# A second product over all 128 partitions: the keys' low part on both halves

## The chip, the cores and the metric

The kernel runs on one core of one Trainium2 chip. The metric is the device time of one execution in microseconds (us), taken several times; times here are those of that one core.

## The reference

Two layers of an encoder trunk over 512 tokens of 1024 channels, in float32. Each layer has two mixers and a channel mixer. Cut to what matters here:

```
z = rms_norm(x) @ w_in          # split into qa ka va, qi ki wi, cq ckv kr, ga gb
# indexer: 8 heads of 64, one shared key
score = sum_h wi[t,h] * relu(qi[t,h] . ki[s]) * scale ; masked by chunks of 64
sel = top_k(score, 128)
# mixer A: 8 heads of 64, RMS-normed queries and keys, softmax over the selected keys
logits = qa[t,h] . ka[s,h] * scale + bias[h, bucket(s - t)]
# mixer B: 8 heads of 96, softmax over all keys of the chunk and before
logits = qb[t,h] . kb[s,h] * scale
x = x + (gate_a * (y_a @ w_proj_a) + gate_b * (y_b @ w_proj_b)) @ w_out
x = x + (silu(conv(gat)) * conv(val)) @ w_down     # of rms_norm(x) @ w_up
```

## The kernel before

Float32 values are split into two parts, a high one (a cast to float32r) and a low one (what is left), and a product of two values is made of several products of parts on TensorE, added up in one PSUM bank. A dense tile of weights takes 24 matmuls of 512 columns (line 513) or 48 of 256 columns (`rows`, line 536).

Weights stream through the class `Weights`: SP's queue loads a raw tile (line 151), ScalarE casts the high part (line 168), VectorE makes the low part (line 177), or a DMA that adds does (line 194). Three raw tiles and four split tiles are held (`WB`). All other operands of 128 x 512 come from one pool of 65 slots.

A layer first computes the projections by tiles as a generator, the filler. Attention work is written as generators too, and `weave` steps them in turn and hands out filler after each step at rates that are constants. VectorE's and ScalarE's follow-up work is put off by `later(n, f)`, where the clock counts steps. So the order of TensorE's work is fixed in the program: in the indexer one step is a head's scores of one query block (two matmuls), then one step of filler (three matmuls). The top-k follows, on VectorE, beside projections and mixer B; then mixer A, four heads a group.

The scores of the indexer and of mixer A use `mm2` (lines 310 to 314). A head's queries are stacked: one half of the 128 partitions holds the high part, the other the low part. The keys' high part stands on both halves, so one product over 128 partitions (line 313) gives high times high plus low times high. The second product (line 314) takes the half that holds the queries' high part, 64 partitions, with the keys' low part on the same half. Which half it is alternates with the head. Widths are 128, 256, 384 and 512 columns by query block in mixer A, and 256, 384 and 512 in the indexer.

The indexer's key (`evac_kiw`, lines 559 to 570) gets its low part on both halves by a VectorE copy (line 569). Mixer A's keys are made in `turn` of `heads` (lines 740 to 756), two heads at a time: ScalarE casts each head's high part on its own half (line 752), a DMA on SP's queue copies it to the other half (line 753), and VectorE makes the low part (line 754) one step later, each head's half into the one tile `kal` of the pair.

Mixer B's scores (lines 1114 to 1116) are three products: high by high over 100 partitions (96 dimensions and 4 that carry the mask), high by low and low by high over 96.

Of the kernel before, what the change touches and what calls it, by code (L numbers as in the profile page):

```python
# [98 lines left out]
def dense_plan():  # L99
    """The weight tiles of a layer in the order of their use: (name, index, columns)."""  # L100
    p = [("qi", m, 1024) for m in range(4)] + [("kiw", 0, 1024)]
    p += [("ckv", j, 1024) for j in range(2)] + [("cq", j, 1024) for j in range(3)]
    p += [("gb", m, 1024) for m in range(GB_0)]
    p += [("kv", 0, 1024), ("uq", 0, 1152)]
    p += [("gb", m, 1024) for m in range(GB_0, GB_1)]
    p += [("kv", 1, 1024), ("uq", 1, 1152)]
    p += [("gb", m, 1024) for m in range(GB_1, 8)]
    for g in range(2):
        p += [(n, 2 * g + half, 1024) for n in ("qa", "ka", "va") for half in range(2)]
        if g == 0:  # L110
            p += [("ga", m, 1024) for m in range(GA_0)]
    p += [("pb", m, 1024) for m in range(4 if PBO == 1 else 0)]
    p += [("ga", m, 1024) for m in range(GA_0, 8)]
    p += [("pb", m, 1024) for m in range(0 if PBO == 1 else 4)] + [("pa", m, 1024) for m in range(4)]
    p += [("wo", m, 1024) for m in range(8)]
    for f0, f1 in FF_PARTS:
        for f in range(f0, f1):
            p += [("uv", f, 1024), ("ug", f, 1024)]
        p += [("dn", 11 * mp + kp, 512) for mp, _, _ in DOWNS[f0] for kp in range(f0 // 2, f1 // 2)]
    return p  # L120
# [7 lines left out]
class Weights:  # L128
    """Streams the dense weights: load, then split into two exact float32r parts."""
# [50 lines left out]
    def split_four(self, i, t, h, o, lag):  # L180
        """Four blocks, 21 11 12 22, to the parts of seven: 11 12 22 and Winograd's four sums."""
        self.sums(i, t)
        self.nc.scalar.copy(h[:, :896], t[:, 128:1024])  # L183
        kp = self.seq[i][1] % 11
        if kp in (DN1 if kp < FS // 2 else DN2):
            self.low_by_dma(t[:, 128:1024], o[:, :896])
            return
        self.later(lag, lambda: self.nc.vector.tensor_tensor(  # L188
            out=o[:, :896], in0=t[:, 128:1024], in1=h[:, :896].bitcast(F32), op=OP.subtract))

    def low_by_dma(self, t, o):
        """The rest of a value, by a DMA that adds it to its first part's negative."""
        self.nc.scalar.activation(o, t, AF.Copy, scale=-1.0)  # L193
        self.nc.gpsimd.dma_start(o.bitcast(F32), t, accum_op=OP.add)  # L194
# [19 lines left out]
    def ahead(self):  # L214
        """Called when the last tile given out has been used: the one after the next takes its place."""
        for j in range(1, WB[1]):
            self.split(self.at + j, 2)
        for j in range(WB[1], WB[1] + WB[0] - 1):
            self.load(self.at + j)
        if PRE and self.at + WB[1] < len(self.seq) and self.seq[self.at + WB[1]][0] == "dn":  # L220
            self.sums(self.at + WB[1], self.raw[self.at + WB[1]])
# [3 lines left out]
def trunk(ctx: ExitStack, tc: tile.TileContext, xT, wd, vecs, rel, rot_n, onehot, outT):  # L225
# [58 lines left out]
    def hi_lo(src, name, scale=None, lag=1):  # L284
        """Splits a whole [128, 512] source into exact parts, with a scale by partition if any."""
        h, o = slot(name + "h", F32R), slot(name + "l", F32R)
        split_into(h, o, src, scale, lag)
        return h, o
# [9 lines left out]
    def stack(p, name):  # L298
        """The parts of two heads of 64, each head's above one another: [high; low] and [low; high]."""
        e, o = slot(name + "e", F32R), slot(name + "o", F32R)  # L300
        A.copy(e[0:64], p[0:64])
        A.copy(o[64:128], p[64:128])

        def low():
            V.tensor_tensor(out=e[64:128], in0=p[0:64], in1=e[0:64].bitcast(F32), op=OP.subtract)
            V.tensor_tensor(out=o[0:64], in0=p[64:128], in1=o[64:128].bitcast(F32), op=OP.subtract)
        later(1, low)
        return e, o

    def mm2(p, q, ts, kk, kl, half, start, stop):  # L310
        """A head's [high; low] queries with its keys: twice the high part, then the low one."""
        r = slice(64 * half, 64 * half + 64)
        mm(p, lhsT=q[:, ts], rhs=kk, start=start, stop=False, skip_group_check=True)  # L313
        mm(p, lhsT=q[r, ts], rhs=kl[r], start=False, stop=stop, skip_group_check=True)  # L314
# [6 lines left out]
    def rsqrt(a, shape, quick=False):  # L321
        """a ** -0.5 by Newton's steps from a first guess by the exponent's bits."""
# [22 lines left out]
    def table(func, out, in_, **kw):  # L345
        """An activation of a function with a table of its own: all of one come before the next one's."""
# [44 lines left out]
    # Columns that mask the later half of a query block's own keys, when they are contracted with each other.  # L391
# [43 lines left out]
    class Norm:  # L435
# [17 lines left out]
        def finish(self, gap):  # L453
            """Mean square plus eps by token, its inverse root, and that over all partitions."""
# [20 lines left out]
        def rescale(self, xs, lag, step):  # L475
            """New parts, of the inputs times their factor."""
# [10 lines left out]
        def after(self, f):  # L487
            """Runs f once the factor is there."""
            if self.waiting is None:
                f()  # L490
            else:
                self.waiting.append(f)
# [26 lines left out]
    def rows(name, grp, nrm, evac):  # L519
        """256 columns of the projection with tokens on partitions; evac(b, p) per two blocks of them."""  # L520
# [29 lines left out]
    def mix_dense(l, nrm):  # L550
        """The dense products of a mixing phase, as the tensor engine's filler."""
# [22 lines left out]
        def turn_wk(wk):  # L574
# [7 lines left out]
            # The indexer's weights by head: |w| and its sign.  # L582
# [12 lines left out]
            # The shared rotary key, turned and scaled.  # L595
# [113 lines left out]
        # Mixer A's queries and keys: by token, normed there, then turned.  # L709
        def heads(name, grp, gain):  # L710
# [30 lines left out]
            def turn(pr):  # L741
# [8 lines left out]
                e, o, low = slot("kae", F32R), slot("kao", F32R), slot("kal", F32R)  # L750
                for t, r, r2 in ((e, slice(0, 64), slice(64, 128)), (o, slice(64, 128), slice(0, 64))):
                    A.activation(t[r], p[r], AF.Copy, scale=gain[r])
                    nc.sync.dma_start(t[r2].bitcast(F32), t[r].bitcast(F32))
                    later(1, lambda t=t, r=r: V.scalar_tensor_tensor(low[r], p[r], gain[r], t[r].bitcast(F32),
                                                                      op0=OP.mult, op1=OP.subtract))
                st["ka"][hd:hd + 2] = (e, low), (o, low)
# [20 lines left out]
        # Mixer B's queries, keys and values of four heads, by token.  # L777
# [156 lines left out]
    class Feeder:  # L934
        """Called after each step of the attention: hands out filler, and side work, at given rates."""
# [25 lines left out]
    def index_scores():  # L961
        st["sc"] = {}
        for i in (3, 2, 1):
# [3 lines left out]
            for h in range(8):  # L967
                p = bank("L")
                ts = slice(i * 128, (i + 1) * 128)
                mm2(p[:, :w], st["qi"][h], ts, st["kih"][:, :w], st["kil"][:, :w], h % 2, True, True)  # L970
# [43 lines left out]
    def values(P, v, half, two):  # L1014
        """v(j): a head's values of key block j, [128 keys, high and low 64]; half: which of the pair's heads."""
# [39 lines left out]
    def bias_a(h):  # L1055
        """A head's bias by distance, and the mask of the keys that were not selected."""
# [12 lines left out]
    def scores_a(h, P):  # L1069
# [5 lines left out]
        for i in range(4):  # L1075
# [3 lines left out]
            mm2(p[:, :w], q, ts, kk[:, :w], kl[:, :w], h % 2, True, not SELPE)  # L1079
# [11 lines left out]
    def turn_b(h):  # L1091
        """A head's queries and keys with their dimensions on partitions."""
# [13 lines left out]
    def scores_b(h, P):  # L1106
# [3 lines left out]
        for i in range(4):  # L1110
# [4 lines left out]
            mm(p[:, :w], lhsT=qh[0:96, ts], rhs=kl[0:96, :w], start=False, stop=False, skip_group_check=True)  # L1115
            mm(p[:, :w], lhsT=ql[0:96, ts], rhs=kh[0:96, :w], start=False, stop=True, skip_group_check=True)
# [6 lines left out]
    def weave(gens, each, others=()):  # L1123
        """Steps the generators in turn, with filler and side work after each step."""
# [33 lines left out]
    for l in range(DEPTH):  # L1158
# [55 lines left out]
        # Mixer B.  # L1214
# [14 lines left out]
        # Mixer A.  # L1229
# [26 lines left out]
        # Gates, output projection.  # L1256
# [25 lines left out]
        # Channel mixer.  # L1282
# [3 lines left out]
        def act_pair(kp, c0, c1):  # L1286
            """The parts of the seven operands of two blocks of the hidden layer, by halves of the tokens."""
# [54 lines left out]
        # Two products a bank; "n" marks an operand, and so a product, of the opposite sign.  # L1342
# [6 lines left out]
        def down(mp, pairs, first, last, then):  # L1349
            """Two blocks of the output: 2 x 2 blocks a time by seven products of Winograd's form of Strassen's."""  # L1350
# [92 lines left out]
def lay_out(i):  # L1443
# [3 lines left out]
    def tiles_t(w):  # L1447
        """[K, 128 columns] -> [128, K]: input blocks beside each other."""
        return w.reshape(-1, 128, w.shape[1]).transpose(1, 0, 2).reshape(128, -1)
# [73 lines left out]
```

## Time and profile before

| what | us |
|---|---|
| median of 3 runs | 1611.2 |
| fastest and slowest of them | 1602.91, 1611.62 |
| the profiled execution, first to last instruction | 1601.6 |
| TensorE (PE) busy | 1584.5 |
| weight loads (PEld) busy | 1339.8 |
| VectorE (DVE) busy | 1117.3 |
| ScalarE (ACT) busy | 953.2 |
| GpSimd (POOL) busy | 413.0 |

The profile is of one execution; its own time is known as the span from its first to its last instruction, and the time outside that span isn't told. Durations of matmuls are modelled at their ends, as matmuls are pipelined: a matmul of 512 columns is shown with about 0.39 us, though the next starts 0.23 us after it. So distances between starts tell TensorE's pace better than durations do. The granted clock of TensorE is 1.000 over the span.

### The profile page before, as it was taken

How to read it: one execution, taken by the hardware profiler on the slowest of the kernel's cores; microseconds unless marked ns; L12 is line 12 of the kernel's file. 1: busy time of each engine (PE TensorE's matmuls, PEld its weight loads, DVE VectorE, ACT ScalarE, POOL GpSimd, SP SyncE). 2: the span in 40 equal slices, each digit the busy share in tenths (PEclk: the TensorE clock that was granted, in tenths of full speed). 3: DMA queues.
4: the chain of work that ended last, by engine and by line, in shares of the span. 5: the costliest groups of instructions: out<-in, count | busy, mean ns of one | idle time of the engine just before them, and what ended most of it. 6: DMA issues, size and time to landing. Idle time of an engine off the chain costs nothing.

```text
span 1601.6 us, 23906 instructions
## 1 busy us (share of the span) xinstructions
PE 1584.5 (99%) x8662; PEld 1339.8 (84%) x8662; DVE 1117.3 (70%) x2271; ACT 953.2 (60%) x1551; POOL 413.0 (26%) x602
## 2 busy tenths in 40 slices
PE   9999999999999999999999999999999999999998
PEld 6688999778888898889976889997788888978898
DVE  7699987656567692547776999876574666825576
ACT  6657676763467545764456576777735675356642
POOL 1235003210012231226801340123000122412276
PEclk9999999999999999999999999999999999999999
DMA  7374122634378538982443731246244884398833
GB/s 239 112 177 119 54 80 80 166 98 145 105 181 194 119 101 206 222 194 81 141 142 80 184 100 53 80 102 162 80 148 120 179 198 108 104 210 202 203 97 105
DMA packets 70983, 219.01 MB, mean 137 GB/s; under 512 B 8192, under 2 KB 8488, under 8 KB 70736
## 3 DMA queue, kind: packets, MB, share of 16 engines
q1 hardware_dynamic: 51968, 147.31, 29.1%
q0 software_dynamic: 18432, 67.38, 22.8%
q10 hardware_dynamic: 464, 2.79, 0.5%
q8 instruction: 68, 1.11, 0.3%
q14 instruction: 51, 0.42, 0.1%
HBM read 143.77 MB, written 6.84 MB: 94 GB/s over the span
## 4 chain that ended last, share of the span: by engine, by line
PE 73%; DVE 7%; POOL 4%; DMA 3%; ACT 2%; issue 2%; POOLq 0%; ACTq 0%; DVEq 0%
PE D L513 37%; PE T L513 14%; PE D L536 7%; PE Y L1030 2%; PE T L1023 2%; DMA wr<-in_wd_dram 2%; PE L L314 2%; POOL wr L205 2%; PE L L1370 2%; PE L L513 1%; DVE wl L188 1%; POOL wr L203 1%; POOL wr L204 1%; PE L L313 1%; DMA wl<-wr 1%
## 5 line engine op out<-in xcount | busy, mean ns | idle before, releaser
L168 ACT CAST wh<-wr 128x1024 fp32r<-128x1024 f32 x202 | 211.8, 1050 | 180.0 <-PE D L513 72.6
L194 POOL DMA_DIRECT2D wl<-wr x128 | 110.7, 867 | 693.0 <-ACT wl L193 638.4
L513 PE MATMUL D<-hxh,wh 128*128 128x512 f32 x464 | 188.4, 406 | 0.1
L513 PE MATMUL D<-hxl,wh 128*128 128x512 f32 x464 | 187.1, 403 | 0.0
L183 ACT CAST wh<-wr 128x896 fp32r<-128x896 f32 x88 | 82.8, 942 | 128.0 <-POOL wr L205 96.9
L193 ACT ACTIVATE wl<-wr 128x1024 fp32r<-128x1024 f32 (+1 forms) x128 | 135.7, 1061 | 30.5 <-PE D L513 21.2
L205 POOL TENSOR_TENSOR wr<-wr 128x256 f32<-128x256 f32 x88 | 109.4, 1243 | 92.9 <-DVE wr L204 83.2
L188 DVE TENSOR_TENSOR wl<-wr,wh 128x896 fp32r<-128x896 f32 x88 | 101.7, 1156 | 43.8 <-ACT wh L183 35.6
L513 PE MATMUL D<-hxh,wl 128*128 128x512 f32 x464 | 127.9, 401 | 0.0
L1065 POOL TENSOR_TENSOR P<-M,sel 128x128 f32<-128x128 f32 (+1 forms) x64 | 53.0, 883 | 269.3 <-DMA M<-skewd 107.2
L536 PE MATMUL D<-wh,hxh 128*128 128x256 f32 x384 | 115.9, 302 | 0.0
L536 PE MATMUL D<-wl,hxh 128*128 128x256 f32 x384 | 109.0, 284 | 0.0
L536 PE MATMUL D<-wh,hxl 128*128 128x256 f32 x384 | 108.8, 283 | 0.0
L513 PEld LDWEIGHTS D<-hxh,wh 128*128 128x128 f32 x464 | 87.5, 189 | 19.9 <-issue 4.3
L513 PEld LDWEIGHTS D<-hxl,wh 128*128 128x128 f32 x464 | 87.4, 188 | 19.7 <-issue 4.8
L177 DVE TENSOR_TENSOR wl<-wr,wh 128x1024 fp32r<-128x1024 f32 x74 | 92.5, 1253 | 12.0 <-ACT wh L168 9.1
L513 PE MATMUL D<-hrl,wh 128*128 128x512 f32 x256 | 99.6, 389 | 0.0
L513 PE MATMUL T<-hrl,wh 128*128 128x512 f32 x256 | 99.6, 389 | 0.0
L513 PE MATMUL D<-hrh,wh 128*128 128x512 f32 x256 | 99.6, 389 | 0.0
L513 PE MATMUL T<-hrh,wh 128*128 128x512 f32 x256 | 99.6, 389 | 0.0
L513 PEld LDWEIGHTS D<-hxh,wl 128*128 128x128 f32 x464 | 83.8, 188 | 17.5 <-issue 2.0
L293 DVE TENSOR_TENSOR ptl<-T,pth 128x512 fp32r<-128x512 f32 (+3 forms) x128 | 61.5, 486 | 25.6 <-ACT pth L292 24.2
(397 smaller groups left out, 4527.0 us busy)
## 6 DMA issues: line engine op xcount, KB each, us to landing
wr<-in_wd_dram SPq DMA_DIRECT2D x198, 512.0 KB, 4.0
wl<-wr POOLq DMA_DIRECT2D x124, 512.0 KB, 5.4
wr<-in_wd_dram SPq DMA_DIRECT2D x88, 256.0 KB, 2.7
x<-in_xT_dram SPq DMA_DIRECT2D x16, 256.0 KB, 4.9
M<-skewd SPq DMA_DIRECT2D x16, 256.0 KB, 3.9
skewd<-biasd ACTq DMA_DIRECT2D x1, 2560.0 KB, 13.3
wr<-in_wd_dram SPq DMA_DIRECT2D x4, 576.0 KB, 3.7
wl<-wr POOLq DMA_DIRECT2D x4, 576.0 KB, 6.4
```

Source lines behind the costliest of these rows:

```text
L168: self.nc.scalar.copy(h[:, :n], t[:, :n])
L177: eng.tensor_tensor(out=o[:, c], in0=t[:, c], in1=h[:, c].bitcast(F32), op=OP.subtract)
L183: self.nc.scalar.copy(h[:, :896], t[:, 128:1024])
L188: self.later(lag, lambda: self.nc.vector.tensor_tensor(out=o[:, :896], in0=t[:, 128:1024], in1=h[:, :896].bitcast(F32), op=OP.subtract))
L193: self.nc.scalar.activation(o, t, AF.Copy, scale=-1.0)
L194: self.nc.gpsimd.dma_start(o.bitcast(F32), t, accum_op=OP.add)
L205: g(2)(out=b[:, 6:8], in0=b[:, 0:3:2], in1=b[:, 3:6:2], op=OP.add)
L293: later(lag, lambda: V.tensor_tensor(out=o, in0=src, in1=h.bitcast(F32), op=OP.subtract))
L314: mm(p, lhsT=q[r, ts], rhs=kl[r], start=False, stop=stop, skip_group_check=True)
L513: mm(p, lhsT=w, rhs=x, start=n == 0, stop=n == len(seq) - 1, skip_group_check=True)
L536: mm(pp[b][:, t, :], lhsT=x, rhs=w, start=n == 0 and half == 0 and t == 0, stop=n == 11 and half == 1, skip_group_check=True)
L1065: G.tensor_tensor(out=P[:, P0[i]:P0[i] + w], in0=M[:, 512 - w:512], in1=sel[:, SEL0[i]:SEL0[i] + w], op=OP.add)
```

## The change

`mm2` loses its argument `half`, and its second product takes all 128 partitions of queries and keys. With the keys' low part on both halves, this adds the product of the two low parts, which was left out before. In the indexer only the call changes. In mixer A each head gets a low tile of its own, and a DMA copies the low part to the other half. Mixer B's second and third product take 100 partitions instead of 96. The diff, without lines that only drop comments:

```diff
-    def mm2(p, q, ts, kk, kl, half, start, stop):
-        r = slice(64 * half, 64 * half + 64)
+    def mm2(p, q, ts, kk, kl, start, stop):
         mm(p, lhsT=q[:, ts], rhs=kk, start=start, stop=False, skip_group_check=True)
-        mm(p, lhsT=q[r, ts], rhs=kl[r], start=False, stop=stop, skip_group_check=True)
+        mm(p, lhsT=q[:, ts], rhs=kl, start=False, stop=stop, skip_group_check=True)
...
-                e, o, low = slot("kae", F32R), slot("kao", F32R), slot("kal", F32R)
-                for t, r, r2 in ((e, slice(0, 64), slice(64, 128)), (o, slice(64, 128), slice(0, 64))):
+                for i, (r, r2) in enumerate(((slice(0, 64), slice(64, 128)), (slice(64, 128), slice(0, 64)))):
+                    t, low = slot("kah", F32R), slot("kal", F32R)
                     A.activation(t[r], p[r], AF.Copy, scale=gain[r])
                     nc.sync.dma_start(t[r2].bitcast(F32), t[r].bitcast(F32))
-                    later(1, lambda t=t, r=r: V.scalar_tensor_tensor(low[r], p[r], gain[r], t[r].bitcast(F32),
-                                                                      op0=OP.mult, op1=OP.subtract))
-                st["ka"][hd:hd + 2] = (e, low), (o, low)
+
+                    def rest(t=t, low=low, r=r, r2=r2):
+                        V.scalar_tensor_tensor(low[r], p[r], gain[r], t[r].bitcast(F32), op0=OP.mult,
+                                               op1=OP.subtract)
+                        nc.sync.dma_start(low[r2].bitcast(F32), low[r].bitcast(F32))
+                    later(1, rest)
+                    st["ka"][hd + i] = t, low
...
-                mm2(p[:, :w], st["qi"][h], ts, st["kih"][:, :w], st["kil"][:, :w], h % 2, True, True)
+                mm2(p[:, :w], st["qi"][h], ts, st["kih"][:, :w], st["kil"][:, :w], True, True)
...
-            mm2(p[:, :w], q, ts, kk[:, :w], kl[:, :w], h % 2, True, not SELPE)
+            mm2(p[:, :w], q, ts, kk[:, :w], kl[:, :w], True, not SELPE)
...
             mm(p[:, :w], lhsT=qh[0:100, ts], rhs=kh[0:100, :w], start=True, stop=False, skip_group_check=True)
-            mm(p[:, :w], lhsT=qh[0:96, ts], rhs=kl[0:96, :w], start=False, stop=False, skip_group_check=True)
-            mm(p[:, :w], lhsT=ql[0:96, ts], rhs=kh[0:96, :w], start=False, stop=True, skip_group_check=True)
+            mm(p[:, :w], lhsT=qh[0:100, ts], rhs=kl[0:100, :w], start=False, stop=False, skip_group_check=True)
+            mm(p[:, :w], lhsT=ql[0:100, ts], rhs=kh[0:100, :w], start=False, stop=True, skip_group_check=True)
```

## The prediction

> **What bounds the kernel now.** I read the page first (busy time), then the waits of TensorE, then the timeline around the instructions that the diff touches, and last the rows of the engines and queues that could take over.
>
> ```profile
> span 1601.6 us, 23906 instructions
> ...
> PE 1584.5 (99%) x8662; PEld 1339.8 (84%) x8662; DVE 1117.3 (70%) x2271; ACT 953.2 (60%) x1551; POOL 413.0 (26%) x602
> ```
>
> TensorE is busy for 99% of the span, and no other engine comes near. A busy PE is not yet a PE at its peak, so two more questions are needed: does PE wait for anybody, and does it run its matmuls at their usual pace? The longest wait of PE in the whole span is the row below (operation, releaser, us in total, times, longest). The two rows after it are the only waits of PE between 85 and 232 us, from the end of the first layer's indexer to the start of its mixer A.
>
> ```profile
> PE L L317 <- ACT hxh L295: 1.7, 1, 1.7
> ...
> PE L L804 <- DVE vb L293: 0.6, 1, 0.6
> PE T L1099 <- DVE qao L306: 0.2, 1, 0.2
> ```
>
> So PE is the bound, and hardly ever kept waiting. The pace is read from the distance between the starts of neighbouring matmuls, in the timeline (start, duration, operation). First a stretch of the indexer:
>
> ```profile
> 46.53 0.39 PE L513 MATMUL D<-hxh,wh 128*128 128x512 f32 x1
> 46.76 0.39 PE L513 MATMUL D<-hxl,wh 128*128 128x512 f32 x1
> 46.98 0.39 PE L313 MATMUL L<-kih,qio 128*128 128x512 f32 x1
> 47.30 0.49 PE L314 MATMUL L<-kil,qio 64*128 64x512 f32 x1
> 47.72 0.50 PE L513 MATMUL D<-hxh,wh 128*128 128x512 f32 x1
> 48.06 0.40 PE L513 MATMUL D<-hxl,wh 128*128 128x512 f32 x1
> ```
>
> Usual matmuls of 512 columns start 0.23 us apart (46.53, 46.76, 46.98). Around line 314, the one with 64 rows, three distances are longer: 0.32 before it, 0.42 after it, 0.34 after the next. Together 1.08 us instead of 3 x 0.23 = 0.69: 0.39 us are lost to one narrow matmul, though PE counts as busy throughout. Is it the 64 rows, or the accumulation into a bank of tag L? Mixer B's scores answer, which accumulate three products in such a bank, the later two with 96 rows:
>
> ```profile
> 225.06 0.40 PE L1114 MATMUL L<-tbh,tbh 100*128 100x512 f32 x1
> 225.29 0.40 PE L1115 MATMUL L<-tbl,tbh 96*128 96x512 f32 x1
> 225.53 0.40 PE L1116 MATMUL L<-tbh,tbl 96*128 96x512 f32 x1
> 225.76 0.28 PE L536 MATMUL D<-wh,hxh 128*128 128x256 f32 x1
> ```
>
> They start 0.23, 0.24 and 0.23 us apart: going from 100 rows to 96 and on to 128 costs nothing. What is slow is the step to 64 rows and the step back.
>
> **The change part by part: the matmul of line 314.** It gets 128 rows, and the three long distances should become usual ones. For the narrower widths, the same reading in mixer A:
>
> ```profile
> 249.71 0.22 PE L313 MATMUL L<-kao,qao 128*128 128x128 f32 x1
> 249.86 0.32 PE L314 MATMUL L<-kal,qao 64*128 64x128 f32 x1
> 250.12 0.39 PE L536 MATMUL D<-wh,hxh 128*128 128x256 f32 x1
> 250.34 0.28 PE L536 MATMUL D<-wh,hxl 128*128 128x256 f32 x1
> 250.46 0.28 PE L536 MATMUL D<-wl,hxh 128*128 128x256 f32 x1
> ...
> 251.66 0.28 PE L313 MATMUL L<-kao,qao 128*128 128x256 f32 x1
> 251.86 0.38 PE L314 MATMUL L<-kal,qao 64*128 64x256 f32 x1
> 252.17 0.39 PE L536 MATMUL D<-wh,hxh 128*128 128x256 f32 x1
> 252.39 0.28 PE L536 MATMUL D<-wh,hxl 128*128 128x256 f32 x1
> ```
>
> Here the usual distance is 0.12 (250.34 to 250.46). With 128 columns: 0.15 + 0.26 + 0.22 = 0.63 against 0.36, so 0.27 us too much. With 256 columns: 0.20 + 0.31 + 0.22 = 0.73 against 0.36, so 0.37. For 384 columns I take 0.38, between the values of 256 and 512. How many there are of each:
>
> ```profile
> L314 PE MATMUL L<-kal,qae x32: 322/408/492, 232.6 to 1126.2; 64*128 64x128 f32 x8, 64*128 64x256 f32 x8, 64*128 64x384 f32 x8, 64*128 64x512 f32 x8
> L314 PE MATMUL L<-kal,qao x32: 323/408/502, 249.9 to 1141.0; 64*128 64x128 f32 x8, 64*128 64x256 f32 x8, 64*128 64x384 f32 x8, 64*128 64x512 f32 x8
> L314 PE MATMUL L<-kil,qie x24: 378/440/498, 45.8 to 873.2; 64*128 64x512 f32 x8, 64*128 64x384 f32 x8, 64*128 64x256 f32 x8
> L314 PE MATMUL L<-kil,qio x24: 379/435/498, 47.3 to 874.9; 64*128 64x512 f32 x8, 64*128 64x384 f32 x8, 64*128 64x256 f32 x8
> ```
>
> That is 16 of 128 columns and 32 of each other width, 112 in all. Indexers (16 of each of three widths, both layers): 16 x (0.37 + 0.38 + 0.39) = 18.2 us. Mixers A (16 of each of four): 16 x (0.27 + 0.37 + 0.38 + 0.39) = 22.6 us. Sum: 40.8 us of PE's time, 2.5% of the span. Rounding of the starts to 0.01 us leaves about 0.03 per matmul, 3.4 us in all.
>
> The Trainium skill has a rule for this row: in "TensorEngine Tiling (Array Packing)", Key Properties, that changing the tiling mode, not just the tile, drains TensorE; and "TensorE: Matmul & The Clock Gate", Single matmul latency, puts a drain at about 175 ns. By that estimate 112 x 2 x 0.175 = 39.2 us would go. The trace agrees in place and size (three long distances, 0.27 to 0.39 us per narrow matmul).
>
> **Mixer B's 96 rows become 100.** 128 matmuls, at the distances quoted above (0.23 and 0.24 with 96 rows, 0.23 with 100). Cost nothing, bounded by +-0.01 x 128 = 1.3 us.
>
> **Indexer's keys.** Their low part stands on both halves already, by the copy in the code's `low` of `evac_kiw`: nothing is added.
>
> **Mixer A's keys.** The low part gets a tile per head instead of one per pair, and is copied to the other half by a DMA on SP's queue, issued after VectorE made it: 16 DMAs of 128 KB (4 pairs x 2 heads x 2 layers). VectorE and ScalarE keep the same instructions. The nearest rows are those of the copy of the high part and of the VectorE step (durations ns min/median/max, first start), and what SP waits for now:
>
> ```profile
> L753 SPq DMA_DIRECT2D kae<-kae x8: 461/467/593, 226.2 to 1084.1; - x8
> DMA to landing us min/median/max: 2.2/4.2/5.0
> ...
> L754 DVE SCALAR_TENSOR_TENSOR kal<-T,gab,kae x8: 732/740/744, 226.8 to 1085.2; 64x512 fp32r<-64x512 f32 x8
> ...
> SPq L151 <- DVE wl L177: 368.2, 64, 12.3
> ```
>
> The tightest use is the first head: its low part is ready at 226.84 + 0.74, about 227.6; with 2.2 to 5.0 us it lands at 229.8 to 232.6, and PE wants it at 232.6. So 0, at worst about 0.5 us a layer (an issue of 0.47 ahead of it). I take 0, nearest to the median of 4.2. The second pair of a group and the other heads follow 17 us or more behind (249.9 is the second head's first use). If that cover were gone, 16 x 4.2 = 67 us would be on the path. The Trainium skill speaks against adding DMAs: "DMA: Bandwidth & Descriptors", Anatomy of one DMA, gives each a fixed cost of about 2.0 us; were all exposed, that estimate takes back 32 us of the gain. The trace has even more per copy (2.2 to 5.0 us), but beside PE's work.
>
> SP's queue: a copy of the low part stands at the head of SP's queue until VectorE's step is done (the high part's was issued at 226.2 + 0.47, VectorE was done at 227.6: about 0.9 us more), and queued behind it are the next pair's copies, the bias load `M` and the weight loads. A weight load is issued for a tile four or five tiles ahead; at 24 x 0.23 = 5.5 us a tile that is 22 us of reserve. Cost nothing. Slots: one more tile per pair; by a count over the program's order at most 59 of the 65 are alive in mixer A, so 63. Cost nothing.
>
> **What is late next.** As PE gets through the indexer sooner, VectorE gets less time for the same work. Columns of the next rows: stretch, its length, busy us of PE, PEld, DVE, ACT, POOL.
>
> ```profile
> 45.00:85.00 40.00, 40.00 (x152) 25.39 (x151) 26.66 (x58) 25.06 (x42) 8.72 (x16) 1.00 0.36 91
> 85.00:125.00 40.00, 39.64 (x185) 33.13 (x184) 39.28 (x124) 24.01 (x44) 14.94 (x39) 1.00 0.76 180
> 125.00:232.00 107.00, 106.31 (x717) 95.87 (x718) 101.12 (x269) 75.08 (x167) 17.38 (x45) 1.00 0.27 77
> ```
>
> The indexer's stretch shrinks by 9.1 us a layer to 30.9, and VectorE's 26.7 us still fit. Behind it, with the top-k, VectorE is full (39.3 of 40). It starts there 9.1 us earlier, but with less slack. I expect the waits that PE has for it there, 0.6 + 0.2 us, to double: 0.8 us a layer, 1.6 in all; the bounds are 0 and all 18.2 us of the indexers. In mixer A there is room: no row of PE's waits lies there.
>
> Sum: 40.8 - 1.6 = 39.2 us. The profiled execution has a span of 1601.6 us, so 1562.4 after. The fastest of the three times is 1602.91 (1.3 us outside the span), the median 9.6 us above it: 1611.2 - 39.2 = 1572.0 us. Less than 8 us (0.5%) either way can hardly be told from no change.
>
> **The rivals.** (1) VectorE becomes the bound between indexer and mixer A and gives the indexers' part back: 40.8 - 18.2 = 22.6 us saved, 1588.6 us. For it: 39.28 of 40 and 101.12 of 107 us busy. Against it: 13.3 idle us of VectorE in the indexer, of which only 9.1 are taken, so that VectorE too should enter the full stretch sooner.
> (2) The loss does not come from the rows but from something that stays, such as the use of the same queries twice in a row: no change, 1611 us. Against it: the rows of mixer B, and that the matmul behind line 314 is late although it belongs to another product.
> (3) Slower: the new copies hold SP, as each waits for VectorE at the head of the queue, and the weight loads behind come too late. The longest wait of SP for VectorE's low parts is 12.3 us; 8 pairs of copies x 12.3 = 98 us, less 40.8: about 1668 us. It decides only if a hold is longer than the reserve: 22 us less 5.0 for a slow landing, 17 us; and more than 40.8 / 8 = 5.1 us of each hold must reach PE. Against it: 12.3 is below 17, and in the rows above VectorE's step began 0.6 us after the issue of the high part's copy (226.2, 226.8).
>
> **How the numbers follow.** Forecast (34 to 43 us saved) 0.73; rival 1 0.19; rival 2 0.05; rival 3 0.03. The range takes in the forecast and rival 1: below, the full 40.8 and its 3.4 of rounding from the fastest time, 1602.9 - 44.2 = 1558.7, so 1559; above, rival 1 from the median, 1589. Faster by over 0.5%: 0.73 + 0.19 = 0.92; same 0.05; slower 0.03.
>
> **What would show it.** In the profile after, the second product has 128 rows and starts 0.23 us (512 columns) or 0.12 us (128, 256) behind the first; the next starts 0.23 behind it. The idle time of the weight loads before it, put down to issue, is gone. 16 new DMAs kal to kal land before their heads' first product. The stretch of each indexer is about 9 us shorter, that of each mixer A about 11. Rival 1 shows as new waits of PE for VectorE in mixer B, rival 3 as waits of PE for weights. I am wrong if the distances stay long at 128 rows, or become usual while the span does not shrink.

## The result, and the profile after

The changed kernel takes 1565.5 us (median of 4 runs, 1562.11 to 1568.42), the kernel before 1608.0 (4 runs, 1602.91 to 1611.62). The ratio is 0.9741, with a 95% interval of 0.9724 to 0.9757: by it 41.6 us or 2.6% less, 39 to 44 by the interval; the two medians are 42.5 us apart. The forecast was 39.2 us less and 1572.0 us, in a range of 1559 to 1589. The profiled execution of after took 1562.11 us, 1.7 of it outside its span. From the page of the profile after:

```profile
span 1560.4 us, 23953 instructions
...
PE 1542.9 (99%) x8662; PEld 1338.8 (86%) x8662; DVE 1116.3 (72%) x2271; ACT 950.4 (61%) x1551; POOL 414.5 (27%) x602
```

The span is 41.2 us shorter. TensorE has as many matmuls as before (8662) and is as full (99%); VectorE and ScalarE do the same work, and their shares rise because the span is shorter. A change that takes 41 us out of TensorE's path and moves its busy share not at all shows how little that share says. In after.py line 312 is the first product of `mm2` and line 313 the second. The timeline of the indexer after the change:

```profile
46.47 0.39 PE L512 MATMUL D<-hxl,wh 128*128 128x512 f32 x1
46.70 0.39 PE L312 MATMUL L<-kih,qio 128*128 128x512 f32 x1
46.92 0.39 PE L313 MATMUL L<-kil,qio 128*128 128x512 f32 x1
47.15 0.39 PE L512 MATMUL D<-hxh,wh 128*128 128x512 f32 x1
47.38 0.39 PE L512 MATMUL D<-hxl,wh 128*128 128x512 f32 x1
```

The three long distances are gone: 0.22, 0.23 and 0.23 instead of 0.32, 0.42 and 0.34 us. With 128 columns in mixer A:

```profile
239.65 0.22 PE L312 MATMUL L<-kah,qao 128*128 128x128 f32 x1
239.72 0.28 PE L313 MATMUL L<-kal,qao 128*128 128x128 f32 x1
239.83 0.33 PE L535 MATMUL D<-wh,hxh 128*128 128x256 f32 x1
240.00 0.28 PE L535 MATMUL D<-wh,hxl 128*128 128x256 f32 x1
```

0.07 + 0.11 + 0.17 = 0.35, where 0.63 stood. Another sign that the prediction names lies in the weight loads (PEld). Before, in the stretch of the indexer that the prediction shows:

```profile
46.76 0.19 PEld L313 LDWEIGHTS L<-kih,qio 128*128 128x128 f32 x1
47.30 0.18 PEld L314 LDWEIGHTS L<-kil,qio 64*128 64x128 f32 x1 [0.35 <-issue]
47.72 0.19 PEld L513 LDWEIGHTS D<-hxh,wh 128*128 128x128 f32 x1 [0.24 <-issue]
```

The first load starts 0.22 us ahead of its matmul (46.98), beside the matmul before it. The load of the narrow product and the one behind it start only with their own matmuls (47.30 and 47.72). The idle time of the loads that the profile puts down to issue was 25.9 us at line 314, 11.1 at line 513 and 2.6 at line 536. After the change 1.0 us is left at line 512 and none at the other two: 38.6 us less, close to what PE gained. So the loss shows itself as weight loads that no longer run beside other matmuls; why they are held, no row says.

Where the time went by stage can be read from the first and last start of the second product (fourth and fifth number of a row), in the first 400 us of before and of after:

```profile
L314 PE MATMUL L<-kal,qae x16: 324/408/492, 232.6 to 329.7; 64*128 64x128 f32 x4, 64*128 64x256 f32 x4, 64*128 64x384 f32 x4, 64*128 64x512 f32 x4
L314 PE MATMUL L<-kal,qao x16: 323/408/502, 249.9 to 344.5; 64*128 64x128 f32 x4, 64*128 64x256 f32 x4, 64*128 64x384 f32 x4, 64*128 64x512 f32 x4
L314 PE MATMUL L<-kil,qie x12: 378/440/498, 45.8 to 78.8; 64*128 64x512 f32 x4, 64*128 64x384 f32 x4, 64*128 64x256 f32 x4
L314 PE MATMUL L<-kil,qio x12: 379/435/498, 47.3 to 80.1; 64*128 64x512 f32 x4, 64*128 64x384 f32 x4, 64*128 64x256 f32 x4
```

```profile
L313 PE MATMUL L<-kal,qae x16: 223/310/397, 223.8 to 311.9; 128*128 128x128 f32 x4, 128*128 128x256 f32 x4, 128*128 128x384 f32 x4, 128*128 128x512 f32 x4
L313 PE MATMUL L<-kal,qao x16: 273/311/397, 239.7 to 325.2; 128*128 128x128 f32 x4, 128*128 128x256 f32 x4, 128*128 128x384 f32 x4, 128*128 128x512 f32 x4
L313 PE MATMUL L<-kil,qie x12: 279/338/389, 46.0 to 70.0; 128*128 128x512 f32 x4, 128*128 128x384 f32 x4, 128*128 128x256 f32 x4
L313 PE MATMUL L<-kil,qio x12: 278/338/389, 46.9 to 71.0; 128*128 128x512 f32 x4, 128*128 128x384 f32 x4, 128*128 128x256 f32 x4
```

The indexer took 34.3 us from its first to its last second product (45.8 to 80.1) and takes 25.0. From there to mixer A it was 152.5 us and is 152.8: a mere 0.3 us is given back on the way. Mixer A took 111.9 us and takes 101.4. The second layer, read the same way, gives 9.3 us less, 0.2 us less and 10.7 us less. Together 39.7 us. Of the other 1.5, 0.6 lie between the two readings (344.5 to 840.5 before, 325.2 to 820.6 after) and 1.1 behind the second, less 0.2 ahead of the first. The distances behind each mixer A's last narrow product, which this reading leaves out, are part of that.

VectorE, which was to be late next, is in fact full in that middle stretch. Busy us of PE, PEld, DVE, ACT and POOL in the stretch between indexer and mixer A, and below them PE's only waits there:

```profile
75.80:116.00 40.20, 39.60 (x185) 32.91 (x183) 40.20 (x126) 23.98 (x44) 14.76 (x38) 1.00 0.78 184
116.00:223.50 107.50, 106.44 (x720) 96.13 (x721) 101.53 (x270) 75.16 (x168) 16.89 (x45) 1.00 0.28 79
```

```profile
PE L L807 <- DVE vb L293: 0.9, 1, 0.9
PE T L1102 <- DVE qao L306: 0.2, 1, 0.2
```

VectorE has no idle time left for 40 us, and still PE waits only 1.1 us in place of 0.8. In the second layer it is 1.7 us in place of 1.5. The new copies and their landing:

```profile
L757 SPq DMA_DIRECT2D kal<-kal x16: 461/496/561, 218.8 to 1055.4; - x16
...
DMA to landing us min/median/max: 2.3/3.7/4.6
```

The first is issued at 218.8 and lands by 223.4 at the latest; its product starts at 223.8.

### The profile page after: what moved, and what is told of

It reads as the page before. It is cut to its first block, busy times and chain, and to the rows that moved or that the text cites. A ratio compares the mean times of both kernels' runs of the same rounds, so it can differ in the third digit from the quotient of the medians.

```text
span 1560.4 us, 23953 instructions
## 1 busy us (share of the span) xinstructions
PE 1542.9 (99%) x8662; PEld 1338.8 (86%) x8662; DVE 1116.3 (72%) x2271; ACT 950.4 (61%) x1551; POOL 414.5 (27%) x602
## 4 chain that ended last, share of the span: by engine, by line
PE 69%; DVE 10%; POOL 4%; DMA 4%; ACT 3%; issue 2%; POOLq 0%; DVEq 0%; ACTq 0%; SPq 0%
PE D L512 37%; PE T L512 14%; PE D L535 6%; DMA wr<-in_wd_dram 2%; PE Y L1033 2%; POOL wr L205 2%; PE T L1026 2%; DVE wl L188 2%; DMA wl<-wr 1%; PE L L1373 1%; POOL wr L204 1%; PE L L313 1%; POOL wr L203 1%; PE L L312 1%; ACT wh L183 1%
## 5 line engine op out<-in xcount | busy, mean ns | idle before, releaser
L512 PE MATMUL D<-hxh,wh 128*128 128x512 f32 x464 | 185.2, 399 | 0.4 <-DVE qio L306 0.4
L512 PE MATMUL D<-hxl,wh 128*128 128x512 f32 x464 | 183.5, 396 | 0.0
```

Of the source, the lines that this page charges most:

```text
L512: mm(p, lhsT=w, rhs=x, start=n == 0, stop=n == len(seq) - 1, skip_group_check=True)
```

## The experiments

Theory A says that the price is paid for going from matmuls of 128 rows to 64 and back. Its rivals: each narrow matmul is slow by itself (B), or the loss belonged to these two products (C). Then come the copies' price and VectorE's reserve. Each kernel was timed in 3 rounds beside the kernel before; its span is that of one profiled execution. Between mixer A and the second layer's indexer, which no edit touches, these executions differ by up to 7 us (495.4 us in after, 502.7 in the slowest). So each edit is also read in its own place, from starts as above.

**One narrow product in mixer B** (from the kernel after):

```diff
-            mm(p[:, :w], lhsT=qh[0:100, ts], rhs=kl[0:100, :w], start=False, stop=False, skip_group_check=True)
+            mm(p[:, :w], lhsT=qh[0:64, ts], rhs=kl[0:64, :w], start=False, stop=False, skip_group_check=True)
```

> The kernel after the change, but in mixer B the second of three products contracts 64 rows instead of 100 (the products of the last 36 rows of the keys' low part are left out). 64 matmuls, 16 of each width, each between two of 100 rows. Theory A, the price is paid for going from 128 rows to 64 and back, by whatever product: 16 x (0.27 + 0.37 + 0.38 + 0.39) = 22.6 us more, a span of 1560.4 + 22.6 = 1583.0 us. Theory B, each matmul of 64 rows is slow by itself: the same 1583.0. Theory C, the loss belonged to the two products of the indexer and mixer A (their keys, their bank) and not to the rows: 1560.4 us.

Measured: ratio to before 0.9851 (0.9832 to 0.987), span 1583.2 us; that the span meets the expected 1583.0 is luck, as 4.6 of the 22.8 us more lie outside the edit's place. After stands at 0.9741, so about 18 us are lost. From the indexer's last second product to mixer A's first (71.0 to 233.0 and 858.2 to 1021.5) it is 162.0 and 163.3 us, where after has 152.8 and 154.3: 18.2 us more in the place of the edit. The timeline:

```profile
147.33 0.23 PE L1117 MATMUL L<-tbh,tbh 100*128 100x128 f32 x1
147.49 0.32 PE L1118 MATMUL L<-tbl,tbh 64*128 64x128 f32 x1
147.74 0.33 PE L1119 MATMUL L<-tbh,tbl 100*128 100x128 f32 x1
147.90 0.45 PE L512 MATMUL D<-hxl,wh 128*128 128x512 f32 x1
148.19 0.40 PE L512 MATMUL D<-hxh,wh 128*128 128x512 f32 x1
```

A product that never had a loss now has one: 0.86 us from first to last start. In after the same five matmuls start at 145.48, 145.54, 145.65, 145.76 and 146.04, which is 0.56, so 0.30 are too much, near the 0.27 of 128 columns in mixer A. C falls. The total is 18 and not 22.6 us, though the loss itself is as large as expected. In 59 of the 64 places the trace of each kernel has the three products and the next two matmuls one behind the other; from first to last start they add up to 61.1 us here and 39.6 in after, 21.4 more. Some of it took the place of waits: PE's idle time between indexer and mixer A is 2.0 us in both layers together, where after has 3.5. That is 1.5 of the 4.4 us that are missing; the rest is open.

**Two narrow products behind each other**: as above, and line 1119 too.

```diff
-            mm(p[:, :w], lhsT=ql[0:100, ts], rhs=kh[0:100, :w], start=False, stop=True, skip_group_check=True)
+            mm(p[:, :w], lhsT=ql[0:64, ts], rhs=kh[0:64, :w], start=False, stop=True, skip_group_check=True)
```

> As the run with one narrow product in mixer B, but the third product has 64 rows too (of it, too, the last 36 rows are left out), so that two matmuls of 64 rows stand behind each other, on the same half. 128 narrow matmuls in 64 pairs. Theory A (price per change of rows): a pair pays once, 22.6 us as with one, 1583.0 us. Theory B (price per narrow matmul): twice, 45.2 us, 1605.6 us. Theory C: 1560.4 us.

Measured: ratio 0.9854 (0.9836 to 0.9871), span 1586.4 us, and 161.8 and 163.2 us in the same stretches: 17.9 us more than after, as with one. The same place of the timeline:

```profile
147.38 0.22 PE L1117 MATMUL L<-tbh,tbh 100*128 100x128 f32 x1
147.53 0.32 PE L1118 MATMUL L<-tbl,tbh 64*128 64x128 f32 x1
147.70 0.27 PE L1119 MATMUL L<-tbh,tbl 64*128 64x128 f32 x1
147.90 0.50 PE L512 MATMUL D<-hxl,wh 128*128 128x512 f32 x1
148.24 0.39 PE L512 MATMUL D<-hxh,wh 128*128 128x512 f32 x1
```

Again 0.86 us from first to last, and 60.5 us in the 59 places where one narrow product has 61.1. Twice the narrow matmuls, the same loss: the price is on the change of rows, and B falls.

**Pairs of heads in the indexer** (from the kernel before; only the order is another):

```diff
-            for h in range(8):
-                p = bank("L")
...
-                mm2(p[:, :w], st["qi"][h], ts, st["kih"][:, :w], st["kil"][:, :w], h % 2, True, True)
+            ts = slice(i * 128, (i + 1) * 128)
+            for h2 in range(0, 8, 2):
+                pp = [bank("L") for _ in range(2)]
+                for j in range(2):
+                    mm(pp[j][:, :w], lhsT=st["qi"][h2 + j][:, ts], rhs=st["kih"][:, :w], start=True, stop=False,
+                       skip_group_check=True)
+                for j in range(2):
+                    r = slice(64 * j, 64 * j + 64)
+                    mm(pp[j][:, :w], lhsT=st["qi"][h2 + j][r, ts], rhs=st["kil"][r, :w], start=False, stop=True,
+                       skip_group_check=True)
...
```

> The kernel before the change, with nothing but the order changed in the indexer: for two heads, both wide products come first and then both products of 64 rows, which lie on different halves. Narrow matmuls as many as before. Theory A (price per change of rows): 12 pairs a layer pay once instead of twice, 24 x 0.38 = 9.1 us less than the kernel before, 1601.6 - 9.1 = 1592.5 us. If the two halves also work at the same time, another 24 x 0.175 = 4.2 us less, 1588.3 us. Theory B (price per narrow matmul): 1601.6 us.

Measured: ratio 0.9916 (0.9896 to 0.9936), 13.5 us less than before (10 to 17); span 1590.6 us, 11.0 less. From the indexer's first product to mixer A's first second product (45.5 to 232.6 and 840.2 to 1029.4 before, 45.7 to 227.4 and 835.0 to 1018.9 here) it is 5.4 and 5.3 us less, 10.7 together. B, which expects no gain, falls again. Between A's two numbers, 9.1 and 13.3, the time does not decide; the timeline does:

```profile
45.90 0.39 PE L971 MATMUL L<-kih,qio 128*128 128x512 f32 x1
46.22 0.50 PE L975 MATMUL L<-kil,qie 64*128 64x512 f32 x1
46.22 0.49 PE L975 MATMUL L<-kil,qio 64*128 64x512 f32 x1
46.64 0.50 PE L513 MATMUL D<-hxl,wh 128*128 128x512 f32 x1
46.98 0.39 PE L513 MATMUL D<-hxh,wh 128*128 128x512 f32 x1
```

Both narrow products start at 46.22, and the distances around them, 0.32, 0.42 and 0.34, are those of a single one: the second costs nothing. A pair still pays 0.09 before and 0.19 after, and 0.11 behind that (46.64 to 46.98), so this order gains less than the change, in which nobody pays. It has a price of its own too: in the next pair the second wide product starts 0.43 us behind the first (48.11, 48.54), as its weight load waits 0.47 us for ScalarE. That can be why the gain is below 13.3.

**The indexer undone** (from the kernel after):

```diff
-                mm2(p[:, :w], st["qi"][h], ts, st["kih"][:, :w], st["kil"][:, :w], True, True)
+                r = slice(64 * (h % 2), 64 * (h % 2) + 64)
+                mm(p[:, :w], lhsT=st["qi"][h][:, ts], rhs=st["kih"][:, :w], start=True, stop=False,
+                       skip_group_check=True)
+                mm(p[:, :w], lhsT=st["qi"][h][r, ts], rhs=st["kil"][r, :w], start=False, stop=True,
+                       skip_group_check=True)
```

> The kernel after the change with the indexer's second product back at 64 rows; mixer A and mixer B as after. Forecast: the indexers' 18.2 us come back, less up to 1.6 us that VectorE had taken of them: 1577.0 to 1578.6 us. Rival 1 (VectorE had taken most of the indexers' part): close to 1560.4 us.

Measured: ratio 0.9839 (0.9822 to 0.9856), 15.8 us more than after, a little less than expected; span 1579.9 us, 19.5 more. In place each indexer takes 34.3 us again, 9.3 and 9.2 more than after, and the stretches from there to mixer A change by 0.2 us at most (152.6 and 154.5). The indexer's share is real and reaches the end; rival 1 falls.

**The copies alone** (from the kernel before: the hunk in `turn` of the change, with `mm2` and all calls as before):

```diff
-                e, o, low = slot("kae", F32R), slot("kao", F32R), slot("kal", F32R)
...
+                    t, low = slot("kah", F32R), slot("kal", F32R)
...
+                        nc.sync.dma_start(low[r2].bitcast(F32), low[r].bitcast(F32))
...
```

> The kernel before the change with mixer A's low parts in a tile per head and the 16 copies to the other half, but all products as before: the copied halves are read by nobody. It prices the copies on SP's queue alone. Forecast: nothing, 1601.6 us within 1. Rival 3 (the copies hold SP's queue and the weights come late): slower, up to 98 us; by the 5.1 us a pair of copies that it needs to undo the gain, 1601.6 + 41 = 1642 us or more. If a copy held PE only at the first head of a layer, up to 2 x 4.2 = 8 us.

Measured: ratio 0.9999 (0.9987 to 1.0012), 10 runs against 13. In its trace the copies land like those of after:

```profile
L758 SPq DMA_DIRECT2D kal<-kal x16: 461/536/676, 227.9 to 1089.6; - x16
...
DMA to landing us min/median/max: 2.3/3.8/4.7
```

Sixteen more DMAs and as many waits at the head of SP's queue cost nothing that can be measured (under 2 us). Rival 3 falls.

**More work for VectorE**, once and twice (from the kernel after; the line is there once or twice):

```diff
+                if i == 3:
+                    V.max(out=spare, in_=st["sc"][i][:, :512])
```

> The kernel after the change with one more maximum over 128 x 512 on VectorE in each of the 16 rounds of the top-k of a layer, its result used by nobody: 16 x 0.695 = 11.1 us of VectorE a layer, in the stretch from the indexer to mixer A, where VectorE had about 6 idle us a layer left (147.7 us less 40.2 and 101.5 busy). If VectorE is the bound of that stretch as soon as those are gone (what is left of rival 1): 2 x (11.1 - 6.0) = 10.2 us more, 1570.6 us. If PE stays the bound through its lead: 1560.4 us, within 2.

Measured: ratio 0.9787 (0.9767 to 0.9807), span 1572.9 us. That span is more than either expectation, but 6.9 us of it lie between the first mixer A and the second indexer. In the places that the edit can touch, the time lies between its two expectations: from the indexer's last second product to mixer A's first it takes 153.7 and 156.2 us, 0.9 and 1.9 more than after, and mixer A 0.4 and 1.8 more, 5.0 in all. How much VectorE was given for that, the starts tell (line 989 is the new maximum):

```profile
90.92 0.69 DVE L989 MAX8 m<-sc 128x8 f32<-128x512 f32 x1
91.52 1.47 DVE L991 MAX8 m<-sc 128x8 f32<-128x512 f32 x3
```

As with matmuls, the next instruction starts before the shown duration is over, here 0.60 us behind a maximum of 0.69. So a maximum costs 0.60 and not 0.695 us, 9.6 us a layer and 19.2 in all, where the expectation counts 22.2. The busy columns of the first layer's stretch:

```profile
76.00:116.00 40.00, 39.46 (x185) 33.08 (x184) 40.00 (x121) 23.92 (x44) 15.63 (x41) 1.00 0.77 186
116.00:225.00 109.00, 107.65 (x722) 95.78 (x720) 108.01 (x285) 74.33 (x166) 15.69 (x42) 1.00 0.27 77
```

VectorE has 1.0 us left of 149. Of the 19.2 us more, 5.0 reach PE; the other 14.2, about 7 a layer, went into idle time there and outside the stretch.

> As the run with one more maximum over 128 x 512 per round of the top-k, but with two: 2 x 16 x 0.695 = 22.2 us more of VectorE a layer, results used by nobody. With one, VectorE had 1.0 idle us left in 149 us of the first layer's stretch, and PE came out of it 1.5 us later than without. If VectorE is now the bound, all of the second 11.1 us a layer shows: about 22 us more than with one, ratio to the kernel before 0.9787 + 22 / 1608 = 0.992. If PE still leads: close to 0.9787.

Measured: ratio 0.9895 (0.9867 to 0.9924), 17 us more than with one. In place, the two stretches take 6.6 and 9.2 us more than after and the two mixers A 4.8 and 3.5 more: 24.1 us, 19.1 more than with one maximum, as much as the second maximum costs at 0.60 us each (19.2). In three of these four places PE's mean granted clock was 0.99, 0.98 and 0.98, which is worth up to 7 us of the 24.1, so the match is in part luck. After the change VectorE has, then, some 7 us a layer in reserve (11 at most, if those 7 us are all the clock's); beyond them it is the bound.

**32 rows and 96 rows** (from the kernel after, in `mm2`; with 96 rows `0:96` in the place of `0:32`):

```diff
-        mm(p, lhsT=q[:, ts], rhs=kl, start=False, stop=stop, skip_group_check=True)
+        mm(p, lhsT=q[0:32, ts], rhs=kl[0:32], start=False, stop=stop, skip_group_check=True)
```

> The kernel after the change, but the second product of the indexer and of mixer A takes 32 rows only, 0 to 31 (the other 96 rows of products with the low part are left out). Theory A (price for going to fewer rows and back, at 64 or less): a loss as with 64 rows, 0.27 to 0.39 us each, 41 us more than after, about 1601 us. If the price grows with the rows that are missing: more than that. If 32 rows cost nothing: 1560.4 us.

Measured: ratio 1.0007 (0.9993 to 1.0021), all of the gain is gone, and the stages are those of before (indexers 34.2, mixers A 111.5 and 111.9 us). The weight loads' idle time put down to issue is back too (25.8, 10.7 and 2.6 us). The timeline of the indexer:

```profile
47.09 0.40 PE L312 MATMUL L<-kih,qio 128*128 128x512 f32 x1
47.41 0.50 PE L313 MATMUL L<-kil,qio 32*128 32x512 f32 x1
47.84 0.50 PE L512 MATMUL D<-hxh,wh 128*128 128x512 f32 x1
48.18 0.39 PE L512 MATMUL D<-hxl,wh 128*128 128x512 f32 x1
```

0.32, 0.43, 0.34: the distances of 64 rows.

> The kernel after the change, but the second product of the indexer and of mixer A takes rows 0 to 95 (the last 32 rows of products with the low part are left out). Theory A, read from mixer B's 96 rows: nothing, 1560.4 us and a ratio of 0.974. If every product of less than 128 rows pays, in proportion to what is missing: half of 41 us, about 1581 us, ratio 0.987.

Measured: ratio 0.977 (0.9752 to 0.9789), span 1566.8 us, a few us above after, far from the 1581 of a proportional price. In place there is no loss: the first second product of mixer A starts at 223.8 as in after, and the last one of that layer at 324.9 (325.2 in after). In the second layer it is 280.5 us from the indexer's first second product to mixer A's last (280.3 in after). What the span has more lies between the two layers' readings, 501.2 us where after has 495.4.

```profile
46.85 0.39 PE L312 MATMUL L<-kih,qio 128*128 128x512 f32 x1
47.09 0.40 PE L313 MATMUL L<-kil,qio 96*128 96x512 f32 x1
47.32 0.40 PE L512 MATMUL D<-hxh,wh 128*128 128x512 f32 x1
```

So the price does not grow with the rows that are missing. It is none at 96 and 100, and the same at 64 and 32.

## Why the prediction was right

- **PE is the bound, and its loss is in the distances.** Right: the distances fell to the usual ones, and 41.2 us left the span where the sum of the rows was 40.8. That they agree to 0.4 us is in part luck, as the rounding of the starts alone was 3.4 us. The stages gave 9.3 and 9.3 us (indexers; 9.1 each was forecast) and 10.5 and 10.7 (mixers A; 11.3 each, with the last tail not in the reading).
- **The cause, rows of mixer B against the narrow ones.** Right, and now shown on the chip: moved to another product the loss comes back there, doubling the narrow matmuls in pairs does not double it, 96 rows are free, and 32 cost what 64 cost. Rival 2 falls with that, and with the distances of after, where the same queries are still used twice in a row. The Trainium skill's rule ("TensorEngine Tiling (Array Packing)", Key Properties: a change of tiling mode drains TensorE) fits these runs in place; that it is a drain, no row shows. The estimate of 39.2 us, from the drain of about 175 ns in the Trainium skill ("TensorE: Matmul & The Clock Gate", Single matmul latency), came within 2 us of the 41.2, in part by luck: it gives 0.35 us to each narrow matmul, while the rows have 0.27 to 0.39 by width, in three distances and not two. That tiles work independently, as the Trainium skill says in "TensorEngine Tiling (Array Packing)", Key Properties, is seen in the two narrow products that start together at 46.22.
- **Mixer B's 96 to 100 rows cost nothing.** Right: no run has this part alone, but in the 59 places read above the starts add up to 39.7 us before and 39.6 after.
- **The copies cost nothing.** Right (0.9999, and landings of 2.3 to 4.6 us that end 0.4 us ahead of the first use). The fixed cost of about 2.0 us in the Trainium skill ("DMA: Bandwidth & Descriptors", Anatomy of one DMA) is given there for DMAs that GpSimd issues, and SP issues these; the shortest landing here is 2.3 us, and none is on PE's path.
- **VectorE takes back 1.6 us.** Too much: PE's waits for it there grew by 0.3 and 0.2 us, and the stretches between indexer and mixer A changed by +0.3 and -0.2 us, so it took back 0.1 to 0.5. That the waits did not double fits VectorE's reserve of about 7 us a layer.
- **The time, 1572.0 us, was 6.5 too high.** 3.2 come from the base: I took 1611.2, the median of three runs, and with a fourth it is 1608.0. The other 3.3 are the saving, 42.5 us between the medians and 41.2 between the spans. More than 1 us of that is VectorE's term; what is left is within the spread of the runs.

## What to carry to other kernels

Read the distance between the starts of neighbouring matmuls, not their busy share: here TensorE was 99% busy with 41 us of loss in it. A matmul over 64 or 32 rows between matmuls over 128 or 100 costs about 0.3 to 0.4 us here; fill the rows up if the operands can be put there out of the path, or else put the narrow ones next to each other, on different halves. Before more is saved in such a stretch, look at who is full beside it: here the next reserve is some 7 us of VectorE a layer. Read that, too, from the distances between starts, as durations count the overlap of neighbours twice.

## What the runs showed of the hardware that was not expected

Executions of one kernel differ by 3 to 9 us, and those of after go with the granted clock: they took 1562.11 us at a mean of 1.000, 1563.07 at 0.999, 1568.42 and 1567.85 at 0.997. In the run with two narrow products the place is in the trace, far from the edit, where the channel mixer goes back to products with weights whose low part comes by a DMA. PE waits there 4.1 us for a late DMA (`wl`), up to 603.3. A stretch of 12 us (after the busy columns: granted clock, DMA share, GB/s):

```profile
600.00:612.00 12.00, 8.71 (x29) 7.05 (x30) 0.00 (x0) 4.01 (x4) 1.50 (x2) 0.72 0.76 179
```

From 601.2 to 608.0 the clock is 0.50, and 1.00 on either side, so the matmuls behind the wait run at half pace for almost 5 us more. In after the same wait is 0.8 us and the clock stays at 1.00. The other traces agree: between its first matmuls and its last, PE stands still for 2.3 to 4.1 us at eleven places in the eleven traces together, and each time the clock goes to 0.50 for 3.4 or 6.8 us. At the four places of 1.9 to 2.1 us it does so once, and once more after a wait of 1.8 us. So one late transfer costs more than itself, and spans of single profiles differ by a few us for a reason that has nothing to do with an edit: hence the readings in place above.
